# A batched chunk scan in a hybrid RWKV-7 / attention trunk: another order of the products in a round, and precedence for the scan over its company

## The chip, the cores and the metric

The kernel runs on one core of a Trainium2 chip. The core has five engines with a program each: TensorE (PE in the profile, with PEld for its weight loads), VectorE (DVE), ScalarE (ACT), GpSimd (POOL) and SyncE (SP, which here only issues DMAs). PE multiplies matrices into PSUM; DVE and ACT take results out of PSUM; DMAs move data between the chip's memory and SBUF. The metric is the device time of one execution in microseconds (us), as the median of some runs. All data is float32.

## The reference

The model is a trunk of two layers over 512 latent tokens and 256 context tokens, width 1024. The even layer runs an RWKV-7 mixing (both directions in time, 8 heads of 64) beside a windowed attention; the odd layer runs two other attentions; each layer ends with a squared-ReLU MLP. Every sub-layer is modulated by vectors that come from a product with `w_ada`. What matters here is the recurrence of RWKV-7, for each head and each of two directions, over the context and then the latent tokens:

```python
def step(state, inp):
    r_t, w_t, k_t, v_t, kk_t, a_t = inp
    sa = jnp.einsum('bhvk,bhk->bhv', state, -kk_t)
    state = (state * w_t[:, :, None, :] + sa[..., None] * (kk_t * a_t)[:, :, None, :]
             + v_t[..., None] * k_t[:, :, None, :])
    return state, jnp.einsum('bhvk,bhk->bhv', state, r_t)
```

and the modulation, which the scan does not need before the end of the layer's mixing:

```python
ml = jnp.split(s_lat @ w_ada[i] + b_ada[i], 6, axis=-1)
mc = jnp.split(s_ctx @ w_ada[i] + b_ada[i], 6, axis=-1)
```

## The kernel before

The kernel is one long program without loops on the chip; Python generators trace it. It goes through an input projection, the RWKV mixing, the output projection and MLP of layer 0, layer 1's projections and attentions, and layer 1's output projection and MLP. The change is in the RWKV mixing.

The recurrence is computed in 12 chunks of 64 tokens (`NCH`), for both directions at once. The 8 heads are handled as 4 pairs `p`; a pair fills the 128 partitions. For each pair there are these pieces:

- `prep(p)` makes the factors: `ar` (AR) and `bk` (BK), scaled by the running decay, and the triangular matrices that the chunk form has to invert (L911, L912). These go through memory (`nscr`) into the layout of a block inverse `N`, `X`. `front(p)` is prep's first part, up to the marker FRONT: norms (L404, L414), the small products L864, running sums (L872, L874).
- The inverse: 31 steps of two DVE instructions each (L948, L949), on 32x32 blocks. The result goes through memory again (`xscr`, `tscr`), and the merge (L968, L976) joins blocks to 64x64 in the tile `XI`.
- `chunks(p)` is the scan. It loads `v` (L994) and works in batches of `NB` = 3 chunks, so 4 batches. For a batch b: `factors` (L1017, L1023, L1031: transposes of BK and AR, and v made mean free; `vr` is v reversed, `BT`, `XA`, `Z` the tiles that ACT fills), `masked` (L1043 into AK, L1050 into BT, each masked by DVE at L1044 and L1051), `own` (L1059), `solved` (L1068, the only one that needs XI), and then, a round later, `local` (L1080 into `Nb`, L1093 into the output `py`), `passed` (L1009, called by `chain`, into MQ by DVE at L1107), and three times `step` (L1122 into `pd`, the state `x` by DVE at L1124, L1129 into `py`). Only the steps form a chain from chunk to chunk.
- `mix_out(p)` (L1172 to L1194) normalises and gates the pair's output and stores it to `mixd`.

While pair p is scanned, a second generator `bg` gives the company of the scan: the inverse of pair p + 1, the output of pair p - 1 and the front of pair p + 2. A third, `ag`, is the modulation for the layers ahead: `ada` loads 512 KB of `w_ada` into one of three buffers `w_raw` (L341), multiplies (L352, tile `ad`), transposes (L361) and adds a bias (`mod`, L363). Each yield of the scan is followed by `RATE3` = 1.8 yields of `bg` and `RATE4` = 0.7 of `ag`. After a pair's scan, `rest()` traces the remaining preparation of pair p + 2 up to READY and the merge of pair p + 1, with `RATE5` = 0.5 yields of `ag` for each.

The order in which each engine gets its instructions is not the order of tracing itself. A scheduler runs through the program with its own model of time; each engine gets, among its instructions whose inputs are ready in this model, the one with the lowest priority number, and the numbers are given in the order of tracing. On the chip every engine then takes its list in order. Buffers are handed out by the same scheduler: PSUM has two tiles of `wide()` (two banks each), which the scan, the merge, the preparation and the output share, one `pad` for the modulation and one `py` and `pd` for the scan. `issue_after` ties some products into a fixed order among themselves.

The rounds of the scan are traced so:

```python
for b in range(nb + 1):
    # of batch b:      factors, masked, own, solved
    # of batch b - 1:  local, passed, step 0, step 1, step 2
    # as: factors, local, masked, passed, own, step 0, solved, step 1, step 2
```

Of the kernel before, what the change touches and what calls it, by code (L numbers as in the profile page):

```python
# [175 lines left out]
def trunk(ctx: ExitStack, tc: tile.TileContext, xT, cT, vec_d, wada, we, wo_in, wout, wf1, wf2, lw2_d, la2_d, lg2_d,  # L176
# [802 lines left out]
            yield  # L979

    NB = 3

    def chunks(p, y, ct, pch, res):

# [26 lines left out]
        def factors(b):  # L1011

            pt = wide()[:, 0:NB * 256].rearrange("p (x h k) -> p h x k", x=2 * NB, h=2)
            BT = B[b]["BT"] = ct.tile([128, 2, 2 * NB, 128], F32, name="BT", bufs=2)
            for d in range(2):
                for i in range(NB):
                    PE.transpose(pt[:, :, d * NB + i], BK[d][:, ch[d][NB * b + i], :], ident)  # L1017
            act(BT[:, :, :, 0:64], pt)
            XA = B[b]["XA"] = ct.tile([128, NB, 2, 128], F32, name="XA", bufs=2)
            pw = wide()  # L1020
            pt = pw[:, 0:NB * 128].rearrange("p (i h k) -> p i h k", i=NB, h=2)
            for i in range(NB):
                PE.transpose(pt[:, i], AR[:, NB * b + i, 0:2].rearrange("p d t -> p (d t)"), ident)  # L1023
            pv = pw[:, 512:512 + NB * 128].rearrange("p (i f) -> p i f", i=NB)
            vr = ct.tile([128, NB, 64], F32, name="vr", bufs=2)
            c0 = BWD[NB * b + NB - 1]
            act(vr[:, ::-1, ::-1], c3(v)[:, c0:c0 + NB])
            for i in range(NB):
                for d in range(2):
                    c = FWD[NB * b + i]  # L1030
                    PE.matmul(pv[half(1 - d), i], vr[:, i] if d else v[:, c * 64:c * 64 + 64], C["cent"], start=True, stop=True)  # L1031
            act(XA[:, :, :, 64:128], pt)
            Z = B[b]["Z"] = ct.tile([128, NB, 2, 2, 64], F32, name="Z", bufs=2)
            for d in range(2):
                act(Z[half(1 - d), :, d].rearrange("p i h v -> p i (h v)"), pv[half(1 - d)])
# [37 lines left out]
        def local(b):  # L1073

            BT, Z = B[b]["BT"], B[b]["Z"]
            pn = wide()[:, 0:NB * 128].rearrange("p (i d v) -> p i d v", i=NB, d=2)
            for i in range(NB):
                for d in range(2):
                    for h in range(2):
                        PE.matmul(pn[half(h), i, d], BT[:, h, d * NB + i, 0:64], Z[:, i, d, h], start=True, stop=True)  # L1080
            N = B[b]["N"] = ct.tile([128, NB, 2, 64], F32, name="Nb", bufs=2)
            act(N, pn)
            for i in range(NB):
                for h in range(2):
                    for d in range(2):
                        c = ch[d][NB * b + i]
                        first = not b and not i
                        o, x, y_ = yp[half(c % 2), h, c // 2], BT[:, h, d * NB + i, 64:128], Z[:, i, d, h]
                        if first:
                            env["y"] = PE.matmul(o, x, y_, start=True, stop=False)  # L1090
                        else:
                            with tc.issue_after(env["y"].ins):
                                PE.matmul(o, x, y_, start=False, stop=False)  # L1093
# [36 lines left out]

        nb = NCH // NB
        for b in range(nb + 1):
            if b < nb:
                factors(b)
                yield
            if b:
                local(b - 1)
                yield
            if b < nb:
                masked(b)  # L1140
                yield
            if b:
                passed(b - 1)
                yield
            if b < nb:
                own(b)
                yield
            if b:
                step(b - 1, 0)
                yield  # L1150
            if b < nb:
                solved(b)
                yield
            if b:
                for i in range(1, NB):
                    step(b - 1, i)
                    yield
        act(y.rearrange("p c (h f) -> p h c f", h=2), yp)
        yield
# [290 lines left out]
    with ExitStack() as p2:  # L1450
        def side(name, n=1):
            return p2.enter_context(pool(name, n, side="right"))
        sts[1], ct, tl, wa = side("st1"), side("ct"), side("tl"), side("wa", 3)
        p2.enter_context(psum(0, 2))
        pch = p2.enter_context(pool("pch", 1, space=PSUM))
        pad = p2.enter_context(pool("pad", 1, space=PSUM))
        mk = lambda: pad.tile([128, 512], F32, name="ad")
        ag = ada(wa, 3, mk, [(0, q) for q in range(4, 12)] + [(1, q) for q in range(12)], nc.sync)
        y = tl.tile([128, 6, 128], F32, name="y")
        for t in early:  # L1460
            if t != QUIET:
                next(ag, None)
        gate = mix_gate(tl)
        for t in until(preps[1], READY):
            next(ag, None)
        for t in preps[0]:
            next(ag, None)
        for p in range(4):
            cg, n = chunks(p, y, ct, pch, res), 0

            def turns(*gs):
                gs = list(gs)
                while gs:
                    for g in list(gs):
                        t = next(g, gs)
                        if t is gs:
                            gs.remove(g)
                        else:
                            yield t

            def behind():
                def out():
                    return mix_out(p - 1, y, gate, tl, res) if p else iter(())
                if p < 3:
                    yield from turns(until(preps[p + 1], MERGE), out(), front(p + 2))
                else:
                    yield from out()
                    for x in mixs[::-1]:
                        x.close()
                    p3w["W"] = ffstream(p3w["x"].enter_context(pool("wp3")), 0)  # L1490
                    m0 = p3w["m0"] = p3w["m"].enter_context(pool("m0"))
                    p3w["last"] = m0.tile([128, T], F32, name="last")
                    yield from bonus(3, tl, res, gate, p3w["last"])
                    mh = m0.tile([128, KT, 256], F32R, name="mh")
                    ml = m0.tile([128, KT, 256], F32R, name="ml")
                    p3w["mh"] = mh, ml
                    for j in range(8):
                        for _ in range(3):
                            yield
                        p3w["W"].ahead(j + 1)  # L1500
                        if j in (5, 6):
                            a, b = ((4, 8), (0, 3))[j - 5]
                            if a:
                                mr = m0.tile([128, 4, 256], F32, name="mr")
                            else:
                                mr = tl.tile([128, T], F32, name="t", bufs=2).rearrange("p (k t) -> p k t", k=3)
                            nc.sync.dma_start(mr, mixd[a:b, :, 0:256].rearrange("k p t -> p k t"))
                            split(mh[:, a:b], ml[:, a:b], mr)
            bg = behind()
            due = [0.0, 0.0]  # L1510
            t = None
            for _ in cg:
                n += 1
                due[0] += RATE3
                due[1] += RATE4
                while due[0] >= 1:
                    due[0] -= 1
                    next(bg, None)
                while due[1] >= 1:
                    due[1] -= 1  # L1520
                    next(ag, None)
            def rest():
                if p < 2:
                    yield from until(preps[p + 2], READY)
                if p < 3:
                    yield from preps[p + 1]
            for t in itertools.chain(bg, rest()):
                due[1] += RATE5
                while due[1] >= 1:
                    due[1] -= 1  # L1530
                    next(ag, None)
        for _ in ag:
            pass
        end = mix_last(3, y, tl, p3w["last"], p3w["gate"], mk)
        next(end)
        split(*(m[:, 3] for m in p3w["mh"]), p3w["last"][:, 0:256])
        for _ in end:
            pass
# [188 lines left out]
    with ExitStack() as p3:  # L1727
# [10 lines left out]
        g = out_ff(0, W, ub, into)  # L1738
# [132 lines left out]
```

## Time and profile before

| | |
|---|---|
| median of 3 runs | 2074.44 us (2070.73 to 2074.55) |
| the profiled execution | 2079.02 us, span 2077.2 us |
| PE busy | 1940.1 us (93%) |
| DVE busy | 1116.6 us (54%) |
| ACT busy | 816.4 us (39%) |
| granted PE clock, mean | 0.964 |

The page divides the span into 40 slices; a digit is the busy share of an engine in tenths. The clock is the share of PE's full clock that was granted. A window row gives, for each engine, the busy time and the number of instructions, then the clock, the busy share of the DMA engines, and GB/s. A timeline row has start, length, engine, line, tiles out<-in, shapes and the count of instructions merged in it; in brackets stands the idle time ahead of it and what ended that. PE records two instructions for each float32 product. A wait row has the waiting instruction, what it waited for, the sum, the number of times and the longest one.

### The profile page before, as it was taken

To read this page: it belongs to the slowest core of one execution; us is meant where nothing else is said; L and a number is where in the kernel's file an instruction comes from. 1 tells how busy PE (TensorE), PEld (TensorE's weight loads), DVE (VectorE), ACT (ScalarE), POOL (GpSimd) and SP (SyncE) were. 2 spreads that over 40 slices of the span, in tenths; PEclk is the share of its full clock that TensorE was granted. 3 is DMA by queue.
4 is the path that set the end of the run, shared out by engine and by line. 5 is a ranking of instruction groups with operands and counts; after the bars stand their busy time and mean duration, and the time that the engine had idled before them with its cause. 6 is when DMAs were issued, how large, how long until landed. Compare 5 with 4: busy or idle time off the path is not lost.

```text
span 2077.2 us, 40236 instructions
## 1 busy us (share of the span) xinstructions
PE 1940.1 (93%) x17276; PEld 1663.0 (80%) x17276; DVE 1116.6 (54%) x1991; ACT 816.4 (39%) x1531; POOL 115.2 (6%) x129
## 2 busy tenths in 40 slices
PE   6999996889879899999999999899999899999997
PEld 4788774676667797888888889898878798888887
DVE  5576567546454468234443444765565566444445
ACT  3466432434325344413221232445686645322232
POOL 1000011001000000000000000001121000000000
PEclk9999997798979999999999999999999999999998
DMA  7421335575643234312221221333111425332221
GB/s 308 154 84 62 108 96 138 186 224 165 187 150 109 78 97 132 102 41 82 72 61 41 72 82 41 101 112 100 37 42 41 133 92 163 102 92 82 88 95 41
DMA packets 112019, 217.64 MB, mean 105 GB/s; under 512 B 38496, under 2 KB 63968, under 8 KB 111328
## 3 DMA queue, kind: packets, MB, share of 16 engines
q1 hardware_dynamic: 96544, 191.73, 29.3%
q10 hardware_dynamic: 15296, 23.33, 3.2%
q8 instruction: 135, 2.21, 0.5%
q14 instruction: 44, 0.36, 0.1%
HBM read 184.36 MB, written 28.05 MB: 102 GB/s over the span
## 4 chain that ended last, share of the span: by engine, by line
PE 73%; DVE 12%; issue 5%; ACT 4%; DMA 4%; POOL 2%; SPq 0%; POOLq 0%; ACTq 0%; DVEq 0%
PE x L1568 43%; PE x L429 11%; PE ax L529 3%; PE ax L510 2%; PE b L492 2%; PE b L493 1%; PE b L1009 1%; PE ad L352 1%; DVE X L949 1%; DMA w_raw<-in_wada_dram 1%; DVE pr L948 1%; PE b L1068 1%; DVE w_lo L226 1%; POOL r L265 1%; DMA w_raw<-in_wf_dram 1%
## 5 line engine op out<-in xcount | busy, mean ns | idle before, releaser
L183 ACT ACTIVATE w_hi<-w_raw 128x1024 fp32r<-128x1024 f32 x183 | 192.3, 1057 | 482.1 <-PE x L1568 361.0
L226 DVE TENSOR_TENSOR w_lo<-w_raw,w_hi 128x1024 fp32r<-128x1024 f32 x181 | 220.9, 1224 | 204.3 <-ACT w_hi L183 203.4
L1568 PE MATMUL x<-fl,w_hi 128*128 128x256 f32 (+1 forms) x864 | 291.6, 339 | 3.9 <-DVE fl L1655 3.9
L1568 PE MATMUL x<-fh,w_lo 128*128 128x256 f32 (+1 forms) x864 | 290.1, 337 | 0.0
L1568 PE MATMUL x<-uh,w_hi 128*128 128x512 f32 (+1 forms) x864 | 287.1, 338 | 3.0 <-ACT uh L183 2.9
L1568 PE MATMUL x<-ul,w_hi 128*128 128x512 f32 (+1 forms) x864 | 287.8, 336 | 0.0
L1568 PE MATMUL x<-uh,w_lo 128*128 128x512 f32 (+1 forms) x864 | 287.4, 335 | 0.0
L1568 PE MATMUL x<-fh,w_hi 128*128 128x256 f32 (+1 forms) x864 | 287.4, 338 | 0.0
L1582 DVE TENSOR_TENSOR oa<-x,oa 128x512 f32<-128x512 f32 (+1 forms) x184 | 103.1, 563 | 207.6 <-PE x L1568 206.9
L429 PE MATMUL x<-uh,w_hi 128*128 128x256 f32 (+1 forms) x560 | 189.6, 339 | 0.9 <-ACT po L183 0.6
L429 PE MATMUL x<-uh,w_lo 128*128 128x256 f32 (+1 forms) x560 | 188.3, 336 | 0.0
L429 PE MATMUL x<-ul,w_hi 128*128 128x256 f32 (+1 forms) x560 | 188.1, 336 | 0.0
L1568 PEld LDWEIGHTS x<-fl,w_hi 128*128 128x128 f32 x864 | 165.2, 191 | 22.0 <-DVE fl L1655 4.5
L1568 PEld LDWEIGHTS x<-fh,w_lo 128*128 128x128 f32 x864 | 164.9, 191 | 17.8
L1568 PEld LDWEIGHTS x<-uh,w_hi 128*128 128x128 f32 x864 | 161.9, 190 | 21.3 <-ACT uh L183 4.0
L1568 PEld LDWEIGHTS x<-fh,w_hi 128*128 128x128 f32 x864 | 162.7, 191 | 19.9 <-ACT fh L183 2.5
L1568 PEld LDWEIGHTS x<-ul,w_hi 128*128 128x128 f32 x864 | 162.7, 189 | 17.7
L1568 PEld LDWEIGHTS x<-uh,w_lo 128*128 128x128 f32 x864 | 162.7, 189 | 17.6
L429 PEld LDWEIGHTS x<-uh,w_hi 128*128 128x128 f32 x560 | 106.8, 191 | 10.1 <-ACT po L183 0.8
L429 PEld LDWEIGHTS x<-uh,w_lo 128*128 128x128 f32 x560 | 106.9, 191 | 9.7 <-issue 1.7
L429 PEld LDWEIGHTS x<-ul,w_hi 128*128 128x128 f32 x560 | 106.8, 191 | 9.1 <-issue 1.2
L1654 DVE TENSOR_TENSOR rl<-rl 128x512 f32<-128x512 f32 (+1 forms) x108 | 59.4, 551 | 72.2 <-ACT fh L183 72.0
(303 smaller groups left out, 3441.8 us busy)
## 6 DMA issues: line engine op xcount, KB each, us to landing
w_raw<-in_wf_dram SPq DMA_DIRECT2D x128, 512.0 KB
w_raw<-in_wada_dram SPq DMA_DIRECT2D x96, 512.0 KB
w_raw<-in_we_dram SPq DMA_DIRECT2D x21, 512.0 KB
w_raw<-in_wo_in_dram SPq DMA_DIRECT2D x18, 512.0 KB
w_raw<-in_wout_dram SPq DMA_DIRECT2D x16, 512.0 KB
hsc<-h ACTq DMA_DIRECT2D x8, 1024.0 KB
scr<-po ACTq DMA_DIRECT2D x21, 384.0 KB
h<-hsc SPq DMA_DIRECT2D x7, 1024.0 KB
```

The costliest lines, as they stand in the source:

```text
L183: return S.activation(o, i, f, **k)
L226: eng.tensor_tensor(o_lo, x, o_hi.bitcast(F32), op=ALU.subtract)
L265: G.tensor_tensor(dst, src, C["mhalf"][:, :n], op=ALU.pow)
L352: PE.matmul(ps[32 * j:32 * j + 32, 0:128], si[:, 2 * kp + k, :], w[:, k, j * 128:(j + 1) * 128], start=kp + k == 0, stop=kp == 3 and k == 1)
L429: PE.matmul(ps[:, 0:b - a], x, y, start=j == 0, stop=j == len(pairs) - 1)
L492: PE.matmul(ps[:, off:off + n], qs, kh, start=True, stop=False)
L493: PE.matmul(ps[:, off:off + n], qs, kl, start=False, stop=True)
L510: PE.transpose(pt[:, (kb - k0) * 128:(kb - k0 + 1) * 128], P[:, kb * 128:(kb + 1) * 128], ident)
L529: PE.matmul(po[h * 64:h * 64 + 64, 0:128], v(h, k), pts[h][:, k], start=k == 0, stop=k == n - 1)
L1568: PE.matmul(o, a, b, start=n == 0, stop=n == len(pairs) - 1)
L1582: tt(oa[:, m, tok], ps, oa[:, m, tok], op=ALU.add)
L1654: tt(r, r, r, op=ALU.mult)
```

## The change

In the rounds, `passed` of the batch before comes right after `factors`, and `local` after `masked`; before it was the other way round. The rest of the order stays: factors, passed, masked, local, own, step 0, solved, step 1, step 2.

The generator of the scan is wrapped: each piece of it is traced under `tc.high_priority(offset=600)`. This gives the instructions traced in it, DMAs, DVE and ACT instructions included, priority numbers lower by 600, as if they had been traced 600 instructions earlier. The scan of a pair has some 620 such instructions, some 155 for a batch. The company and the modulation keep their numbers, and the rates at which they are traced stay.

```diff
     NB = 3
+    AHEAD = 600
...
         nb = NCH // NB
         for b in range(nb + 1):
-            if b < nb:
-                factors(b)
-                yield
-            if b:
-                local(b - 1)
-                yield
-            if b < nb:
-                masked(b)
-                yield
-            if b:
-                passed(b - 1)
-                yield
-            if b < nb:
-                own(b)
-                yield
-            if b:
-                step(b - 1, 0)
-                yield
-            if b < nb:
-                solved(b)
-                yield
-            if b:
-                for i in range(1, NB):
+            for old, new in ((None, factors), (passed, None), (None, masked), (local, None), (None, own)):
+                if new and b < nb:
+                    new(b)
+                    yield
+                if old and b:
+                    old(b - 1)
+                    yield
+            for i in range(NB):
+                if b:
                     step(b - 1, i)
+                    yield
+                if not i and b < nb:
+                    solved(b)
                     yield
...
             bg = behind()
             due = [0.0, 0.0]
             t = None
-            for _ in cg:
+            def first_of(g):
+
+                while True:
+                    with tc.high_priority(offset=AHEAD):
+                        if next(g, g) is g:
+                            return
+                    yield
+            for _ in first_of(cg):
                 n += 1
                 due[0] += RATE3
                 due[1] += RATE4
```

## The prediction

> **What bounds the kernel now.** I read the slices of the page first, to find where TensorE (PE) is not full.
>
> ```profile
> span 2077.2 us, 40236 instructions
> ...
> PE   6999996889879899999999999899999899999997
> ...
> PEclk9999997798979999999999999999999999999998
> ```
>
> A slice is 2077.2 / 40 = 51.9 us. Outside the first slice, PE and its granted clock are both short of full mainly in slices 7 to 13, that is from about 310 to 675 us: the stage with the chunk scan. The changed code runs there and nowhere else. Next I cut this stage at the first transposes of `factors(0)` of each head pair (369, 472, 575 and 653 us), plus the hole ahead of pair 0.
>
> ```profile
> core 0: us, PE busy (x) PEld busy (x) DVE busy (x) ACT busy (x) POOL busy (x), PEclk, DMA share, GB/s
> 352.00:362.00 10.00, 1.09 (x20) 0.48 (x9) 2.62 (x6) 0.00 (x0) 1.10 (x2) 0.50 0.83 160
> 369.00:472.00 103.00, 92.12 (x1903) 70.43 (x1904) 52.66 (x123) 38.33 (x74) 7.56 (x5) 0.88 0.65 202
> 472.00:575.00 103.00, 90.05 (x1843) 70.13 (x1839) 56.78 (x125) 38.05 (x73) 11.13 (x7) 0.90 0.60 178
> 575.00:653.00 78.00, 64.25 (x1410) 52.47 (x1412) 39.30 (x97) 25.07 (x54) 3.62 (x2) 0.87 0.36 106
> 653.00:716.00 63.00, 54.49 (x1086) 44.38 (x1083) 29.61 (x39) 31.35 (x54) 2.28 (x1) 0.92 0.35 113
> ```
>
> From 369 to 716 us PE is busy 92.12 + 90.05 + 64.25 + 54.49 = 300.9 of 347 us. VectorE (DVE) has 178 us of work in the same time. So the stage is bound by PE's own work, which the change does not touch (no instruction is added or dropped), and the most an order can win is the 46 us of idle time, the hole before 369 us, and what the low clock costs. Which waits make the idle time (us in total, times, longest):
>
> ```profile
> PE ad L352 <- DVE mod L363: 7.5, 3, 4.1
> PE ad L352 <- DMA w_raw<-in_wada_dram: 6.0, 9, 1.5
> PE pd L1122 <- DVE MQ L1107: 5.7, 8, 2.3
> ```
>
> The first two, 13.5 us, stand in front of the modulation's matmuls (`ad`, L352), which the change puts behind the scan. The third stands inside the scan's own round.
>
> **Part 1: precedence, the late load of v.** The third stage has a hole of its own, seen in windows of 10 us.
>
> ```profile
> 360.00:370.00 10.00, 7.95 (x213) 7.28 (x214) 0.75 (x4) 3.82 (x8) 0.00 (x0) 0.50 0.90 235
> ...
> 570.00:580.00 10.00, 9.06 (x211) 7.44 (x209) 0.56 (x2) 3.70 (x7) 0.00 (x0) 0.50 0.83 223
> 580.00:590.00 10.00, 4.87 (x58) 2.63 (x50) 3.58 (x4) 0.28 (x1) 3.62 (x2) 0.67 0.38 122
> 590.00:600.00 10.00, 6.72 (x102) 5.08 (x102) 9.07 (x31) 3.10 (x8) 0.00 (x0) 0.76 0.76 248
> ```
>
> Its cause is in the timelines of SyncE's queue and of ScalarE (ACT):
>
> ```profile
> 574.35 11.65 SPq L341 DMA_DIRECT2D w_raw<-in_wada_dram  x3
> 586.05 0.42 SPq L994 DMA_DIRECT2D v<-scr  x1
> ```
>
> ```profile
> 591.32 0.62 ACT L183 ACTIVATE vr<-v 128x192 f32<-128x192 f32 x2 [5.40 <-DMA v<-scr]
> ```
>
> Pair 2's `v`, the first thing that `chunks` traces, is issued behind three loads of the modulation that take the queue 11.65 us (the buffers of `wa` come free late). The centring matmuls of `factors(0)`, then `own(0)`, `solved(0)` and all that follows wait for it; meanwhile PE stands at a modulation matmul:
>
> ```profile
> 590.44 2.79 PE L352 MATMUL ad<-w_raw,si 128*32 128x128 f32 x48 [4.08 <-DVE mod L363]
> ```
>
> With the change this load's place is earlier by up to 600 numbers, ahead of loads traced in the stretch before it. The gain is at most the idle time of these 20 us, 20 - 4.87 - 6.72 = 8.4 us, and what the clock cost, 4.87 x 0.33 + 6.72 x 0.24 = 3.2 us: 11.6 us. At least it is nothing: the load may stay late, or pair 3 may bind instead. For the latter the rows are the last load of pair 3's inverse and its merge:
>
> ```profile
> 625.72 0.52 SPq L961 DMA_DIRECT2D xw<-tscr  x1
> ```
>
> ```profile
> 646.98 0.95 PE L968 MATMUL b<-xw,XI 32*32 32x32 f32 x48
> ```
>
> The merge starts 21 us after its input was asked for; a load here takes some 5 us (586.05 to 591.32), so about 16 us of slack stand behind pair 2, more than 11.6. I take 9.
>
> **Part 2: precedence, the merges.** `factors(0)`, `masked(0)` and `own(0)` of a pair need `ar`, `bk` and `v`, not the inverse, yet they stand behind the merge in PE's order. Ahead of pair 0 that is a plain wait:
>
> ```profile
> 360.59 0.42 PE L968 MATMUL b<-xw,XI 32*32 32x32 f32 x4 [7.92 <-DMA xw<-tscr]
> ...
> 368.96 1.54 PE L1017 MATMUL b<-con,bk 128*128 128x128 f32 x6
> ```
>
> The transposes from 368.96 us on (1.54) and `masked(0)`'s products, L1043 and L1050 (0.58 and 0.90 in the round below), could fill the hole before 360.59: 3.0 us. At the other merges PE stands mainly at the modulation, 6.0 us of waits for its weights in all. Bounds: 0, if the merge is still listed first because the scheduler takes its data to be there, and 9.0. I take 5, about half.
>
> **Part 3: the other order in a round.** Pair 3 shows it without company:
>
> ```profile
> 693.81 0.27 PE L1122 MATMUL pd<-x,MQ 64*64 64x64 f32 x2 [0.39 <-DVE MQ L1107]
> ...
> 700.22 0.58 PE L1043 MATMUL b<-ar,bk 64*64 64x64 f32 x24 [0.20 <-ACT Z L183]
> 700.62 0.90 PE L1050 MATMUL b<-ar,bk 64*64 64x64 f32 x48
> ...
> 704.95 0.38 PE L1122 MATMUL pd<-x,MQ 64*64 64x64 f32 x5 [0.39 <-DVE MQ L1107]
> ...
> 713.25 0.27 PE L1122 MATMUL pd<-x,MQ 64*64 64x64 f32 x2 [1.08 <-DVE MQ L1107]
> ```
>
> ```profile
> 703.93 0.96 DVE L1107 TENSOR_TENSOR MQ<-b,wc 128x768 f32<-128x768 f32 x1 [1.39 <-PE b L1009]
> ```
>
> A round takes 704.95 - 693.81 = 11.14 us, of which 0.39 + 0.20 = 0.59 are waits. `passed` before `masked` and `local` gives MQ (0.96) all of them as cover, so 0.39 goes, and the 0.20 before L1043 is covered by `passed`. But the two `wide` buffers turn: `masked`'s second product, L1050, now takes the buffer that MQ reads, 0.96 us after `passed`, and only L1043 (0.40 from its start to L1050's) lies between. A new wait of 0.56 us, with `local`, `own` and the steps queued behind it on PE. Twelve rounds (three full ones in each of four pairs) give 12 x (0.59 - 0.56) = 0.4 us. In the last round there is no `masked`: `local` covers MQ and the 1.08 us go, in pair 3 for sure. Bounds: -0.56 x 12 = -6.7 and 0.59 x 12 + 1.1 = 8.2. I take 1, as the clean rows have it.
>
> **Part 4: what precedence costs.** The scan's DVE work (AK, BT, MQ, x) now meets the inverse in rounds with less PE work between them.
>
> ```profile
> L948 DVE TENSOR_TENSOR pr<-X,N 96x31 f32<-96x31 f32 (+15 forms) x31 | 10.5, 338 | 1.0
> L949 DVE TENSOR_TENSOR X<-X,pr 96x31 f32<-96x31 f32 (+15 forms) x31 | 10.5, 337 | 1.0
> ```
>
> An inverse is 21 us of DVE work, some two rounds long; the six DVE results of a round that PE waits for can each stand behind one 0.34 us instruction, 2 us a round, 4 us an inverse, 12 us for the three in this stage. Today's 5.7 us of waits for MQ are partly this already. Bounds 0 and -12; I take -3, since precedence also moves these six ahead of inverse steps that are ready.
>
> **Sum.** 9 + 5 + 1 - 3 = 12 us. The profiled execution took 2079.0 us (span 2077.2), so it would take 2067; the median of the runs, 2074.4, lies 4.6 lower: 2062 us.
>
> **The rivals.** A. *The clock comes back too.* The clock is low around the merges: busy time x (1 - clock) in the windows at 360 and 570 us is 7.95 x 0.50 and 9.06 x 0.50, 4.0 and 4.5 us; for four merges at that rate 17 us, about half of what the four stage rows lose in the same way (11.1 + 9.0 + 8.4 + 4.4 = 33 us). If the 32x32 matmuls of the merges are mixed with the next pair's full-size transposes and the clock stays up, the time is 2062 - 17 = 2045. For it: pair 3's stage, with the least beside the scan, has the highest clock, 0.92. Against: at 570 us PE was busy 9.06 of 10 us and had 0.50, so a full PE alone does not keep it. [...]
>
> B. *Nothing is gained in the end.* Work that is put behind the scan comes back: PE's 301 us stay, the loads of the modulation set the pace of the stretches between the scans, or the order on PE hardly moves because its list follows readiness and not the numbers. Then 12 us shrink to one or two: 2073. For it: PE is already 87% busy. Against: the hole at 580 us is no lack of work.
>
> C. *The preparation is starved, slower.* `behind` carries `front(p + 2)`, whose products lead to the inverse of pair p + 2. If pair 1's scan now keeps pair 3's front waiting for its whole length, four rounds or 44.6 us, the 16 us of slack before pair 3's merge are used up and PE waits 28 us, with the gain of 15 us from parts 1 to 3 set against it: 2074 + 13 = 2087. It decides for slower once the front is late by more than 16 + 15 = 31 us. For it: the precedence is as long as a whole pair's scan. Against: the front's instructions were traced up to a pair earlier, so 600 numbers cover only part of them, and each wait in the scan lets them in.
>
> **How the numbers follow.** The forecast has 0.50 (own range 2050 to 2070), A 0.14, B 0.16, C 0.20. Best of all parts, 11.6 + 9.0 + 8.2 = 28.8 and the clock's 17, is 2029; worst, -6.7 - 12 with no gain, 2093. Leaving out about one in ten at each end: 2036 to 2088. About 0.2% (4 us) is what a measurement here can tell from no change; faster is the forecast, A and a little of B, 0.67; same 0.13; slower 0.20.
>
> **What would show it.** Part 1: pair 2's `v` issued before 560 us and no window under 7 us busy around its start. Part 2: L1017 of pair 0 ahead of L968, or not. Part 3: a wait of about 0.5 us of L1050 for MQ in each clean round, none of L1122 for MQ. Part 4: PE's waits for AK, BT and MQ over 8 us in sum. A: clock over 0.9 at the merges. C: the merge of pair 3 waiting for `xw`. The forecast is wrong if PE's idle time in the stage does not fall by some 10 us, or if other stages move.

## The result: slower by 3.1%

The changed kernel takes 2137.1 us (median of 3 runs, 2136.44 to 2139.94) against 2074.4 us before: a ratio of 1.0312, with an interval of 1.0288 to 1.0335. The forecast was 2062 us, and its range ended at 2088. So 62.7 us were lost where 12 were to be won.

The page of the changed kernel, the slices that answer to those of before:

```profile
span 2134.6 us, 40224 instructions
...
PE   5999996898999789999999999999999899999997
...
PEclk9999997896998899999999999999999999999998
```

A slice is 53.4 us now. The low digits still stand mainly where the scan is, in slices 7 to 15 now (320 to 800 us), and PE does not look any emptier there. The windows of this stage of the changed kernel, cut at the first transposes of each pair (columns: window, length, PE busy and its number of instructions, clock, DMA share, GB/s):

```profile
366.00:483.00 117.00, 106.78 (x1755) 0.86 0.44 138
483.00:602.60 119.60, 106.97 (x1862) 0.84 0.52 159
602.60:698.00 95.40, 86.12 (x1559) 0.90 0.50 146
698.00:774.00 76.00, 62.02 (x1072) 0.95 0.23 74
```

The stage is 408.0 us long where it was 347. PE's busy time is 106.78 + 106.97 + 86.12 + 62.02 = 361.9 us where it was 300.9, with 6248 records against 6242. So the idle time is 408.0 - 361.9 = 46.1 us, the same 46.1 as before, and all of the 61 us lie in *busy* time of PE, for almost the same products. The clock is the smaller part of it, by an estimate: busy time x (1 - clock) is 14.9 + 17.1 + 8.6 + 3.1 = 43.7 us over the four rows, against 33 before.

Which products became dearer shows in the groups by line. The kernel before, from 369 to 716 us (busy, mean ns of one | idle before):

```profile
L1050 PE MATMUL b<-ar,bk 64*64 64x64 f32 x768 | 18.1, 232 | 4.2 <-ACT Z L183 2.2 <-issue 0.7 <-DVE AK L1044 0.7
L1009 PE MATMUL b<-BT,XA 64*64 64x128 f32 x352 | 15.0, 286 | 0.0
...
L1080 PE MATMUL b<-Z,BT 128*64 128x64 f32 x384 | 14.7, 224 | 0.1
```

The same three in the changed kernel, from 366 to 774 us (`passed`, `masked`'s second product, and `local`'s first):

```profile
L1010 PE MATMUL b<-BT,XA 64*64 64x128 f32 x352 | 33.8, 300 | 0.6 <-ACT XA L183 0.6
L1051 PE MATMUL b<-ar,bk 64*64 64x64 f32 x768 | 32.0, 239 | 3.0 <-DVE MQ L1108 2.6 <-DVE t L1171 0.3 <-ACT XI L183 0.2
...
L1081 PE MATMUL b<-Z,BT 128*64 128x64 f32 x384 | 27.6, 240 | 2.8 <-DVE AK L1045 2.3 <-DVE BT L1052 0.3 <-ACT Z L183 0.2
```

One product is hardly longer (286 to 300 ns, 232 to 239, 224 to 240). The group is: 15.0 to 33.8, 18.1 to 32.0, 14.7 to 27.6 us. Busy time merges products that run at once: `passed` has 352 x 0.286 = 100.7 us of records in 15.0 us of busy time before, and 352 x 0.300 = 105.6 us in 33.8 now. So a group that costs twice as much has lost its overlap. (Groups that run at the same time are each counted in full, so the differences are no shares of the 61 us.) How they ran before, from PE's timeline of the kernel before in pair 3:

```profile
698.45 0.87 PE L1080 MATMUL b<-Z,BT 128*64 128x64 f32 x24
699.15 0.87 PE L1093 MATMUL py<-Z,BT 128*64 128x64 f32 x24
```

And in the changed kernel, in pair 3, where nothing else competes:

```profile
737.13 0.43 PE L1032 MATMUL b<-con,v 128*64 128x128 f32 x2
737.49 0.43 PE L1010 MATMUL b<-BT,XA 64*64 64x128 f32 x2
737.85 0.43 PE L1032 MATMUL b<-con,vr 128*64 128x128 f32 x2
```

Before, the 24 records of `local`'s first group start within 0.70 us, 58 ns for a product (two records). Now a product of `factors` (tiles of 128*64) and one of `passed` (64*64) take turns, and each takes 0.36 us. The profile shows no wait of PE for another engine in these rows.

The order is not as the text of the change reads. Each piece of the scan is traced in a block that begins at the count of the moment less 600 and sets the count back when it ends. So the scan's own instructions never advance the count. The next piece begins again near the same number, not behind the last of the piece before, and the products of neighbouring pieces whose data is there are sorted into each other, product by product. I counted the neighbours in the list of PE's records from 352 us to the last product into `py`. Before, 285 neighbours differ in the size of their tiles; in the changed kernel 499 do. That gives 62.7 / 214 = 0.29 us for each added change of size, and (61.0 - 10.7) / 214 = 0.24 without the clock's part.

### The profile page after: what moved, and what is told of

It reads as the page before. It is cut to its first block, busy times and chain, and to the rows that moved or that the text cites. A ratio compares the mean times of both kernels' runs of the same rounds, so it can differ in the third digit from the quotient of the medians.

```text
span 2134.6 us, 40224 instructions
## 1 busy us (share of the span) xinstructions
PE 1995.6 (93%) x17276; PEld 1688.9 (79%) x17276; DVE 1113.9 (52%) x1991; ACT 816.9 (38%) x1531; POOL 114.9 (5%) x129
## 4 chain that ended last, share of the span: by engine, by line
PE 78%; DVE 7%; issue 5%; ACT 4%; DMA 3%; POOL 1%; SPq 0%; POOLq 0%; ACTq 0%; DVEq 0%
PE x L1565 44%; PE x L429 10%; PE ax L529 3%; PE ax L510 2%; PE b L1010 2%; PE ad L352 2%; PE b L492 2%; PE b L493 1%; PE b L1069 1%; PE b L1081 1%; PE b L1032 1%; DMA w_raw<-in_wout_dram 1%; POOL r L265 1%; PE py L1094 1%; PE b L1018 1%
## 5 line engine op out<-in xcount | busy, mean ns | idle before, releaser
L183 ACT ACTIVATE P<-b,nmx 128x768 f32<-128x768 f32 (+4 forms) x112 | 82.3, 735 | 38.0 <-DVE nmx L498 26.3
```

Source lines behind the costliest of these rows:

```text
L183: return S.activation(o, i, f, **k)
```

## The experiments

The theories, by the letters that the expectations use. M: the pieces are mixed on PE, and changes between tiles of two sizes cost PE's time. S: the precedence starves other work (rival C of the prediction, and its kin). O: the new order of the round costs the time. Ratios are to the kernel before in the same set of runs, whose median was 2071 to 2073 us in all three sets.

**The two halves alone.** `e1_order` has only the new order of the rounds, without the block of precedence:

```diff
+            for old, new in ((None, factors), (passed, None), (None, masked), (local, None), (None, own)):
...
-            for _ in first_of(cg):
+            for _ in cg:
```

> Before with the new order in the round alone, no precedence. Theory M (mixed pieces: under the precedence every piece starts its numbers anew, some 600 below the present count, which the scan's own instructions do not advance, so two pieces share numbers and PE's list alternates between them; every change between 128*64 and 64*64 tiles costs PE time): no mixing here, so 2068 to 2078 us. Theory S (starvation: the precedence holds up the company of the scan, and the pairs wait for it): no precedence, so the same 2068 to 2078 us. Theory O (the new order of passed and local, with its wait for MQ's buffer, is what costs): 2125 to 2140 us.

`e2_prec` has only the precedence, with the rounds of before:

```diff
-            for _ in cg:
+            for _ in first_of(cg):
```

> Before with the precedence of 600 alone, the old order in the round. Theory M: pieces mixed as in the changed kernel, 2120 to 2150 us. Theory S: 2120 to 2145 us. Theory O: 2060 to 2078 us.

Measured: `e1_order` 2073.2 us, ratio 0.9995 (0.9980 to 1.0011); `e2_prec` 2134.5 us, ratio 1.0287 (1.0259 to 1.0314). The order is neutral, and the precedence is the loss, all but 3 us of it (2137.1 - 2134.5), less than the intervals can tell. O falls. PE's waits in `e1_order`, from 369 to 716 us:

```profile
PE b L1050 <- DVE MQ L1107: 3.8, 8, 1.6
```

That is the wait that part 3 foresaw (0.56 us a round; 3.8 / 8 = 0.48 here), in the place of the 5.7 us of L1122, of which no wait for MQ is left. In `e2_prec` I count 501 changes of tile size.

**Keeping the pieces in order.** `e3_running` lets the numbers run on from piece to piece:

```diff
+                at = tc.cur_priority - AHEAD
                 while True:
-                    with tc.high_priority(offset=AHEAD):
-                        if next(g, g) is g:
-                            return
+                    with tc.high_priority(offset=tc.cur_priority - at):
+                        end = next(g, g) is g
+                        at = tc.cur_priority
+                    if end:
+                        return
```

> The changed kernel, but the priority numbers of the scan run on from piece to piece: the first is 600 below the count at the pair's start, and each piece goes on where the last one ended. The scan still comes ahead of its company by 430 to 600 numbers, but its pieces are not mixed. Theory M: the loss is gone, 2055 to 2085 us, with PE's float32 products in whole groups again. Theory S: precedence as before, 2120 to 2140 us. Theory O: 2120 to 2140 us.

`e4_tied` keeps the precedence as it is, but queues PE's products of each piece behind the last product of the piece before:

```diff
+                        if last is not None:
+                            held.enter_context(tc.issue_after(last))
                         if next(g, g) is g:
                             return
+                        last = [i for i in nc.cur_bb.bb.instructions if i.engine == mybir.EngineType.PE][-1]
```

> The changed kernel with its restarting numbers, but on PE every piece of the scan is queued behind the last matmul of the piece before it (no wait, only the order of issue). The other engines' lists are made with the numbers of the changed kernel. Theory M: PE's groups are whole, 2055 to 2090 us; if it stays above 2110 us, the mixing hurts through DVE, ACT or the PSUM buffers and not through PE's changes of tile. Theory S and theory O: 2120 to 2140 us.

Measured: `e3_running` 2092.2 us, ratio 1.0078 (1.0052 to 1.0104), with 355 changes; `e4_tied` 2074.4 us, ratio 1.0004 (0.9982 to 1.0025), with 292 changes. The precedence is in force in both, so S cannot explain that 45 and 63 us of the loss are gone. Neither gains, though, and `e3_running` lies 7 us above the range that M gave it. In `e3_running` the scan is still mixed at its edges, with the modulation's products, which have numbers of their own:

```profile
640.00 0.41 PE L352 MATMUL ad<-w_raw,si 128*32 128x128 f32 x2
640.33 0.32 PE L1130 MATMUL py<-x,MQ 64*64 64x64 f32 x2
...
649.08 1.08 PE L352 MATMUL ad<-w_raw,si 128*32 128x128 f32 x16 [2.85 <-DMA w_raw<-in_wada_dram]
```

Behind that the modulation, which was put off, waits for its weights. I read its 0.8% (19.5 us) as these two things together and did not separate them. At 0.25 us, the price that `e5_probe` shows below, the 70 added changes would by themselves come to an estimated 18 us. The windows of `e4_tied`, pairs 0 and 1:

```profile
366.16:454.50 88.34, 80.06 (x1738) 0.93 0.54 173
454.50:570.56 116.06, 99.50 (x1861) 0.81 0.53 169
```

Pair 0 takes 88 us in the place of 103, and pair 1 takes 116 in the place of 103: idle time 16.6 us against 13.0, clock 0.81 against 0.90. The records of the modulation (tile `ad`) are 395, 478 and 298 in pairs 0, 1 and 2, where they were 544, 446 and 166: work that was put off comes back, as in rival B. Of the 13 us that pair 1 lost, though, some 10 are the clock's, by the estimate of busy time x (1 - clock) (99.50 x 0.19 = 18.9 us against 90.05 x 0.10 = 9.0), and why the clock is lower there is not shown.

**Mixing without precedence.** `e6_zero` is the changed kernel with an offset of nothing. The block then gives no precedence and still sets the count back:

```diff
-    AHEAD = 600
+    AHEAD = 0
```

> The changed kernel with AHEAD at 0: the scan is still asked for inside the block of precedence, but with no precedence, so that its numbers begin at the count of the moment and the count is set back after each piece; the work traced next gets the same numbers. M (mixed pieces) expects PE's list to be mixed still, now of scan and modulation and inverse as well as of neighbouring pieces, and a time near the changed kernel's or above it, 2110 to 2190 us. S (starvation: the precedence itself holds up the other work) expects the loss to go with the precedence, 2068 to 2080 us. O (the new order of a round costs the time) is out by the run of the order alone and would expect 2137 us.

Measured: 2187.2 us, ratio 1.0568 (1.0524 to 1.0612), 50 us above the changed kernel itself. S would have it at 2068 to 2080. I count 752 changes: (2187.2 - 2071.0) / (752 - 285) = 0.25 us for each added one. The clock is not the cause here, as the stage in one window shows (0.93, against 268 / 300.9 = 0.89 before, by the sum below):

```profile
369.00:821.00 452.00, 415.15 (x6228) 0.93 0.38 120
```

Busy time x clock, an estimate of PE's work at full clock, is 415.15 x 0.93 = 386 us, against 300.9 - 33 = 268 before (33 us is what the clock cost there). The difference of 118 us is again 0.25 for each added change. PE's timeline of `e6_zero`, with transposes of 128*128 by turns with steps of 64*64:

```profile
446.52 0.33 PE L1018 MATMUL b<-con,bk 128*128 128x128 f32 x1
446.78 0.33 PE L1130 MATMUL py<-x,MQ 64*64 64x64 f32 x2
447.04 0.33 PE L1018 MATMUL b<-con,bk 128*128 128x128 f32 x1
```

**The price of a change, by itself.** `e5_probe` is the kernel before with 168 products added in the second layer's MLP, whose results are not used: 24 on tiles of 128*64, 24 on 64*64, then 24 of each by turns; then 24 on 64*64 of half the width, and 24 pairs of the two widths by turns, all on 64*64:

```diff
+            for _ in range(24):
+                full(64)
+            for _ in range(24):
+                quad(128)
+            for _ in range(24):
+                full(64)
+                quad(128)
+            for _ in range(24):
+                quad(64)
+            for _ in range(24):
+                quad(128)
+                quad(64)
```

> Before with 168 idle float32 products put into layer 1's MLP, where the clock is full: 24 on a 128*64 tile (64 columns), 24 on 64*64 tiles (128 columns), 24 of each by turns, 24 on 64*64 tiles with 64 columns, and 24 of each kind of 64*64 by turns. Their results are not used. Theory M (a change between tile shapes costs PE time): the third stretch takes 47 changes x 0.14 us = 6.6 us more than the first and second together (about 1.0 and 0.9 us), that is 8 to 9 us, and the last one, by turns but of one shape, no more than its two kinds alone, about 1.5 us. Against M: the third takes 2 us.

One run, 2093.2 us, beside 2073.4 for the kernel before. The windows of `e5_probe`: the two whole groups, and the stretch by turns in two parts:

```profile
1868.12:1869.67 1.55, 1.55 (x50) 1.00 0.27 50
1869.67:1871.14 1.47, 1.47 (x52) 1.00 0.95 315
1871.14:1877.00 5.86, 5.86 (x43) 0.99 0.56 177
1877.00:1891.27 14.27, 14.27 (x58) 0.50 0.12 38
```

And its PE timeline, early and late in the stretch, and the stretch of one size behind it:

```profile
1871.14 0.33 PE L1582 MATMUL x<-con 128*64 128x64 f32 x2
1871.40 0.43 PE L1587 MATMUL x<-con 64*64 64x128 f32 x2
1871.76 0.33 PE L1582 MATMUL x<-con 128*64 128x64 f32 x2
...
1877.60 0.47 PE L1582 MATMUL x<-con 128*64 128x64 f32 x2
...
1878.62 0.47 PE L1582 MATMUL x<-con 128*64 128x64 f32 x2
...
1891.27 4.81 PE L1587 MATMUL x<-con 64*64 64x128 f32 x146
```

The same 48 products take 1.55 + 1.47 = 3.0 us whole and 5.86 + 14.27 = 20.1 us by turns. At full clock a pair takes 1871.76 - 1871.14 = 0.62 us, against (1.55 + 1.47) / 24 = 0.126 whole: 0.49 us for two changes, 0.25 for each. (In the stretch by turns the products of a kind write to one half of the partitions, where those of the whole groups change halves. That is not the cause: in `e9_alternate` below they change halves as in the scan, and a pair takes the same 0.62 us.) Then the granted clock falls to half, and a pair takes 1.02 us. Turns between two widths of the *same* tile size cost nothing that shows: the last row's 146 records, 73 products, take 4.73 us until the next line starts, 65 ns for each, part of it at the low clock. I had expected 8 to 9 us for the mixed stretch, by the intervals in the changed kernel's trace. The direction was right and the size was too low by more than half.

**The price in the kernel.** `e8_whole` is a control without precedence: it traces `local`'s products into `Nb` directly ahead of those of `passed`, each group whole, and keeps them so. `e9_alternate` differs from it only in that the products of the two groups come by turns:

```diff
-    ALTERNATE = False
+    ALTERNATE = True
...
             todo = [x for n in range(len(ln)) for x in ln[n:n + 1] + pp[n:n + 1]] if ALTERNATE else ln + pp
```

> Before without any precedence, with local's products into Nb traced at passed's place, ahead of passed's own products on 64*64 tiles, each group whole and the whole sequence tied in this order on PE. Local's products into py come after passed. A control for the next kernel. All theories: 2065 to 2085 us.

> The control e8_whole with one difference: local's 12 products (128*64 tiles) and passed's 12 (8 in a pair's first batch; 64*64 tiles) are issued by turns on PE. No precedence, the same work and the same waits. Theory M: 84 changes of tile shape a pair, 336 in all, at (0.199 + 0.152) / 2 - 0.037 = 0.14 us each by the changed kernel's trace: 47 us slower than the control, 2110 to 2130 us. Theory S and theory O: as the control, within 5 us.

Measured: `e8_whole` 2063.1 us, ratio 0.9943 (0.9925 to 0.9961); `e9_alternate` 2193.1 us, ratio 1.0576 (1.0556 to 1.0595). PE's timeline of `e8_whole`, the two groups:

```profile
687.72 0.92 PE L1010 MATMUL b<-Z,BT 128*64 128x64 f32 x24
688.57 0.89 PE L1010 MATMUL b<-BT,XA 64*64 64x128 f32 x24
689.38 0.45 PE L1138 MATMUL py<-Z,BT 128*64 128x64 f32 x8
```

And of `e9_alternate`, the same groups, early and late in them:

```profile
702.56 0.33 PE L1010 MATMUL b<-Z,BT 128*64 128x64 f32 x2
702.82 0.43 PE L1010 MATMUL b<-BT,XA 64*64 64x128 f32 x2
703.18 0.33 PE L1010 MATMUL b<-Z,BT 128*64 128x64 f32 x2
...
709.04 0.69 PE L1010 MATMUL b<-BT,XA 64*64 64x128 f32 x2
...
710.07 0.69 PE L1010 MATMUL b<-BT,XA 64*64 64x128 f32 x2
```

The two groups take 689.38 - 687.72 = 1.66 us whole. By turns a pair takes 0.62 us, as in the probe, and from about 709 us on it takes 1.03. The 659 - 335 = 324 added changes cost 130.0 us, 0.40 each, where 47 us in all had been expected. That is above the 0.25 of full clock because the clock is lower too, as the scan's stage in one window shows, first of `e9_alternate`, then of `e8_whole`:

```profile
366.00:831.00 465.00, 438.52 (x6324) 0.80 0.38 119
```

```profile
366.00:700.00 334.00, 302.96 (x6282) 0.91 0.53 164
```

Busy time x clock is 438.52 x 0.80 = 350.8 us against 302.96 x 0.91 = 275.7. The difference, 75.1 us, is 0.23 for each added change, near the probe's 0.25. The rest is the lower clock, for idle time fell (26.5 us against 31.0). The estimate is somewhat low, since a pair by turns at half clock takes 1.65 times as long (1.02 against 0.62 us in the probe) and not twice. The two kernels hold the same instructions without any precedence, and only the order of these products differs, so this is the price of order alone. It is twice the changed kernel's loss. That the control beat the kernel before was not foreseen. It did so with 50 changes more than before, between whole groups, so the count alone is no price.

**Part 1 alone.** `e7_vload` is the kernel before with the precedence on one instruction:

```diff
-        nc.sync.dma_start(v, scr[3 + 3 * p + 2])
+        with tc.high_priority(offset=600):
+            nc.sync.dma_start(v, scr[3 + 3 * p + 2])
```

> Before with the precedence of 600 on the load of v alone (part 1 of the prediction by itself). If part 1 was right: pair 2's v issued before 560 us, and 2074 - 9 = 2065 us (2063 to 2070). If the backlog gives it back (rival B): 2072 to 2076 us.

Measured: 2062.9 us, ratio 0.9946 (0.9930 to 0.9963), 10.5 us won. The load of pair 2 is issued 59 us earlier (586.05 before), in SyncE's timeline of `e7_vload`:

```profile
527.19 0.34 SPq L995 DMA_DIRECT2D v<-scr  x1
```

And where pair 2 begins, PE is busy at full clock in the windows of 10 us (4.87 and 6.72 us busy before, at 0.67 and 0.76):

```profile
570.00:580.00 10.00, 7.92 (x160) 1.00 0.13 45
580.00:590.00 10.00, 9.96 (x228) 1.00 0.64 206
```

The hole is gone. Not all of its time stays won where it was, though. By the first transposes (367.53, 467.30, 565.69 and 640.42 us), pairs 0, 1 and 2 are each about 4 us shorter than before, and the span of this execution is 18 us under the span of before where the medians differ by 10.5. The edit moves the loads of all four pairs (pair 1's is issued at 428.37 us, before at 445.25). So the gain is shown by the medians, and its sharing out among the pairs, pair 2's hole among them, is not.

**The control and the load together.** `e10_both` has the round of `e8_whole` and the precedence for the load of `v`.

> The round of the control (the two groups of products of local and passed, each whole, back to back) and the precedence for the load of v alone, together. If both gained 11 us by different means, the sum is 2074 - 22 = 2052 us. If the control gained because its load of v for pair 2 came earlier as well (546 us in its trace, 586 us before), the two are one gain and the time stays at 2060 to 2064 us.

Measured: 2061.5 us, ratio 0.9948 (0.9930 to 0.9967). The two gains do not add up; they behave as one. In the control the load of pair 2 was issued early without having been asked to (SyncE's timeline of `e8_whole`):

```profile
546.10 0.38 SPq L995 DMA_DIRECT2D v<-scr  x1
```

So `e7_vload`, one line, has all that was found: faster than the kernel before by 0.5%, and than the changed one by 3.5% (2062.9 against 2137.1).

## Why the prediction was wrong, step by step

**The step that failed** is the sentence that the stage is "bound by PE's own work, which the change does not touch (no instruction is added or dropped)". The first half was right. The second half took PE's busy time as a sum over products, whatever their order. It is a sum over groups: a product of the scan costs about 0.06 us inside its group (58 ns in `local`'s first group before) and about 0.3 us beside one of another tile size (0.36 us in the rows of the changed kernel, 0.62 / 2 = 0.31 in `e5_probe`). Half of this stood in the prediction's rows, the low cost in whole groups: 24 records in 0.58 us and 48 in 0.90 (L1043 and L1050). The price beside another size stood in none of them. The failed sentence stands beside a second assumption, that the block moves the scan's numbers down in one piece ("earlier by up to 600 numbers"). They are moved piece by piece from a count that the scan does not advance. `e4_tied` removes the mixing and not the precedence, `e6_zero` the precedence and not the mixing, and `e9_alternate` mixes without any such block: all three side with M.

The runs put 0.25 us at full clock on a change between 128*64 and 64*64, product by product (`e5_probe`). Why such a change costs time they do not show.

**Part 1** was right in what it moved and in its total: 9 us forecast, 10.5 measured alone. That the 9 come from pair 2's hole is not shown, since in `e7_vload` pairs 0, 1 and 2 are shorter by about as much each, so the close agreement is in part luck. In the changed kernel the load did come early, and what that won was outweighed. SyncE's timeline has the load for pair 2 now 35 us ahead of its transposes in PE's (11 us behind them before), though 7 us after the mark of 560 us:

```profile
567.44 0.34 SPq L995 DMA_DIRECT2D v<-scr  x1
```

```profile
358.92 0.42 PE L968 MATMUL b<-xw,XI 32*32 32x32 f32 x4 [8.00 <-DMA xw<-tscr]
...
366.54 1.54 PE L1018 MATMUL b<-con,bk 128*128 128x128 f32 x6
...
602.58 0.88 PE L1018 MATMUL b<-con,bk 128*128 128x128 f32 x6
```

**Part 2** did not happen: of the 5 us forecast, nothing. The merge of pair 0 still stands ahead of the transposes (358.92 and 366.54) and waits 8.00 us, as it waited 7.92. The lower bound that was given, the merge listed first, is what came. The waits for the modulation's weights, 6.0 us that this part hoped to win back, rose to 11.3 (the first row of the waits below).

**Part 3** was right in its mechanism: the new wait of L1050 is there at 0.48 us. Its size, about 1 us, is too small to be told from nothing (`e1_order`, within 0.2%). **Part 4**, more waits for DVE, did not come. PE's waits in the changed kernel from 362 to 775 us:

```profile
PE ad L352 <- DMA w_raw<-in_wada_dram: 11.3, 10, 2.8
...
PE b L1051 <- DVE MQ L1108: 2.6, 2, 1.4
...
PE b L1081 <- DVE AK L1045: 2.3, 6, 1.0
...
PE b L968 <- DMA xw<-tscr: 0.7, 1, 0.7
```

With the smaller ones the waits for DVE's AK, BT and MQ come to 6.7 us, under the 8 that would have marked it; before they were 14.3, counted in the same way, so the mark was set too low. The last row is rival C's: the merges after pair 0's wait 0.7 us for `xw`, so the inverses were not starved. **C** named the right sign for a reason that is not there. **A** fell as well: at pair 0's merge the clock is still 0.50 (358 to 368 us), at pair 2's it is 0.83 (592 to 602 us) and not the 0.9 that A asked for, and the mean is 0.962 against 0.964. **B** was seen only in `e4_tied`, once the mixing was gone.

The mark given for a wrong forecast, idle time that does not fall by 10 us, did show it (46.1 and 46.1), but neither the forecast nor a rival let the *busy* time rise for the same work, and so the worst sum ended at 2093.

## What to carry to other kernels

Before work is moved on an engine, ask what its order does to the cost of the work, and not only to the waits: where busy time rises with the same number of products, look at neighbours in the engine's timeline. Keep products of one tile size together in groups (here 1.66 us whole in `e8_whole` against more than 7.5 by turns in `e9_alternate`, from 702.56 to 710.07 us), and tie them in order when a planner is free to sort them. A precedence is best given first to the one late instruction that the trace names; here the load of `v` alone had all the gain that was found, and a block around a whole generator reordered everything inside it.

## What the runs showed of the chip

Where products of 128*64 and 64*64 tiles come by turns, a change costs 0.25 us at full clock (`e5_probe`: 0.62 us for a pair by turns, 0.126 whole), and turns within one tile size cost nothing that shows (65 ns for a product there, against 1.47 / 24 = 61 ns in the whole group of the wider ones). In the kernels with added changes, busy time x clock rises by an estimated 0.23 to 0.25 us for each (`after`, `e6_zero`, `e9_alternate`). After about 6 us of turns the granted clock fell to half, in the probe (turns from 1871.14 us on, clock 0.99 until 1877.00 and 0.50 from there to 1891.27) and in `e9_alternate` (turns from 702.56 us on, clock 1.00 from 704.00 to 708.70 and 0.52 from there to 713.00), while the profile has the probe's PE busy for 14.27 of 14.27 us. Turns alone do not settle it: `e6_zero` has the most changes and 0.93 in its stage. In the changed kernel the clock is lower than before in pairs 0 and 1 (0.86 and 0.84 against 0.88 and 0.90) and higher in pairs 2 and 3 (0.90 and 0.95 against 0.87 and 0.92).

The prediction's row at 570 us, 9.06 of 10 us busy at 0.50, is no stretch of turns: only 6 neighbours in it differ in tile size. What lowers the clock there stays open.

Left open: what sets the clock, how cheap a change between whole groups is (the 50 added ones of `e8_whole` cost nothing that its time shows), and how the 0.8% of `e3_running` divides between changes and the modulation's late weights.
